# Modulation vectors of a two-block model: from products on TensorE to multiply-adds on VectorE

## The chip, the cores and the metric

The kernel runs on one core of a Trainium2 chip. A core has TensorE (matrix products into PSUM), VectorE, ScalarE, GpSimd, and SyncE, whose queue issues the loads. The metric is device time in microseconds, the median of several runs; lower is better.

## The reference, cut to what matters

The model is a first block (feed-forwards, an mLSTM mixer, dilated attention, all on 512 tokens of width 1024) and a second block of two layers. Each layer of the second block begins with a modulation that depends on two vectors alone, `c` for the latent tokens and `c_ctx` for the 256 context tokens:

```python
shift, scale, gate       = split(silu(c)     @ w_mod + b_mod, 3)   # w_mod: [1024, 3072] per layer
shift_c, scale_c, gate_c = split(silu(c_ctx) @ w_mod + b_mod, 3)
h_lat = x   * (1 + scale[:, None]) + shift[:, None]
h_ctx = ctx * (1 + scale_c) + shift_c
...                                    # projections, recurrence, two attentions: y_l, y_c
x   = layer_norm(alpha * x   + gate[:, None] * y_l)
ctx = layer_norm(alpha * ctx + gate_c * y_c)     # layer 0 only
```

So per layer a 1024 x 3072 matrix is multiplied by two vectors, in float32: 12 MB are loaded for 2 x 3072 numbers.

## The kernel before, in words

**Layout.** Activations lie feature-major, eight tiles of 128 features by 512 tokens (256 for the context). Large projections run on TensorE as three products of 12-bit parts: a weight tile is loaded into a `raw` buffer, ScalarE copies its high part out, VectorE subtracts to get the low part (`loadw`, `split`), and `mm3` issues low x high, high x low, high x high. A feed-forward weight tile of 128x1024 is split in two halves of 512 columns and gives 24 products of 512 columns.

**Order.** The program is recorded first. `par` weaves independent parts: the first feed-forward `ffn(1, 0)` with `ctx_in(0)` (whose first step is `modulation(0)`) and `mem_kv(0)`; the third, `ffn(1, 1)`, with `ctx_in(1)` and `mem_kv(1)`. A list schedule (`schedule`, `simulate`) with an estimated cost per operation then fixes the order of issue on all engines and a numbered buffer per tile, for the whole program at once. Buffers are few: 4 `raw` (4 KB a partition), 70 `t` (2 KB a partition), 8 PSUM banks `ps`. Each engine runs its list in order and waits by semaphores. Every instruction is issued in `emit`, so that the profile shows line 568 for all of them, and they are told apart by tile kind and shape: `raw` <- `in_wmod_dram` is a load of modulation weights, `ps<-raw,const 128*32` a modulation product, `ps<-t,t 128*128 128x512` a feed-forward or projection product.

**The modulation.** `setup2` puts 0.5 (tanh(c/2) + 1) c for both vectors into the first two of 32 columns of `self.sc`, the others being zero. `modulation(l)` takes the 24 tiles of 128x1024 of `w_mod` (three blocks of 1024 columns, eight row tiles each). Blocks 0 and 1 share a PSUM bank, block 2 has its own. Of each row tile the columns are cut into four, and each quarter is a product of its own on one of four column tiles of TensorE:

```python
self.mm(ps[32 * c:32 * c + 32], self.sc[:, k], w[o // 1024][:, o % 1024:o % 1024 + m],
        start=(k == 0), stop=(k == KD - 1))
```

with m = 512 for the first two blocks and 256 for the third. The 32 output rows are c, c_ctx and zeros. ScalarE copies the sums out, TensorE transposes them, VectorE adds `b_mod`.

Of the kernel before, what the change touches and what calls it, by code (L numbers as in the profile page):

```python
# [14 lines left out]
ALU = mybir.AluOpType  # L15
AX = mybir.AxisListType
P = 128
T = 512
KD = 8
# [4 lines left out]
# ------------------------------------------------------------------ host layouts  # L24
# [5 lines left out]
def _wt(w, ksplit=1):  # L30
    """[K, M] -> [M/128, ksplit, 128, K/128/ksplit*128]: one contiguous block per load."""
    k, m = w.shape
    a = w.reshape(ksplit, k // P // ksplit, P, m // P, P).transpose(3, 0, 2, 1, 4)
    return a.reshape(m // P, ksplit, P, -1)


def _wk(w):
    """[K, N] -> [128, K/128*N]: k tiles side by side."""
    k, n = w.shape
    return w.reshape(k // P, P, n).transpose(1, 0, 2).reshape(P, -1)  # L40
# [71 lines left out]
def _rot():  # L112
    """The lhsT of the rope rotation [-x2, x1, -x4, x3] in each half of 64."""
    m = np.zeros((P, P), np.float32)
    for o in (0, 32, 64, 96):
        for j in range(16):
            m[o + 16 + j, o + j] = -1.0
            m[o + j, o + 16 + j] = 1.0
    return m
# [11 lines left out]
def _order(strict):  # L131
    """[128 = (half, beta or eta, i), direction, head parity, chunk of pair, t]: i up to t in the direction's order, in
    the half that holds the chunk; strict: i before t, and eta alone."""
# [28 lines left out]
def _masks():  # L162
    """Selectors of the first block, loaded where they are used."""
# [7 lines left out]
def pack(a):  # L171
    """Lays the inputs out for the chip: permutations, paddings and copies only."""
# [25 lines left out]
    # second block: tiles r3 k3 v3 dd|ad, rg3, aq3, ak, ag3, nq2, nk2, ng2; token-major av|nv  # L198
    q6 = np.arange(384).reshape(6, 64)[[0, 3, 1, 4, 2, 5]].reshape(-1)
    for l in range(2):  # L200
# [9 lines left out]
        # [3 blocks, 8 k tiles, 128, 1024]  # L210
# [22 lines left out]
def _dil_bias(rel):  # L233
    """[4 heads, 128 queries, 512]: previous and own block of group 0, group 1, group 2; entries of rel_bias or NEG."""
# [11 lines left out]
# neighbourhood attention: tokens in the order (column, row); a tile of 128 queries (16 columns) sees 256 keys from here  # L246
# [3 lines left out]
def _na_bias(rpb):  # L250
    """[2 pairs of heads, 4 tiles, 128 queries, 2 x 256 keys]: entries of rpb, or NEG outside the window of columns."""
# [10 lines left out]
# ------------------------------------------------------------------ recording, order and on-chip memory  # L262
# The program is recorded first, as operations on named tiles. A list schedule over estimated times then fixes the
# order in which the operations are issued, and for every tile one of the numbered slots of its kind.
# [27 lines left out]
class Ref:  # L292
    """A recorded tile, or a view of it. v: numbers of the cells it covers, a cell being a column of 32 partitions."""
# [43 lines left out]
class Recorder:  # L337
    """Stands for the NeuronCore: notes (engine, method, arguments) in the current list."""
# [15 lines left out]
class Op:  # L354
# [9 lines left out]
    def _cost(self):  # L364
        """Estimated microseconds on the engine."""
# [25 lines left out]
def weave(parts):  # L391
    """One order for independent lists of operations, each spread evenly by cost."""
# [9 lines left out]
def dependences(ops):  # L402
    """For each operation the earlier ones that it has to follow."""
    writer, readers, last_pe = {}, {}, {}     # per tile: the last writer of each cell; reads since: (operation, cells)
# [36 lines left out]
def simulate(ops, before, after, key, lag, ahead):  # L441
    """A list schedule: of the operations that are ready and whose tiles have slots, each engine takes the one of least
    key. Only the one of least key overall may take the last slots. lag(i, j): time from the end of i to the start of j."""
# [6 lines left out]
    empty = {k: [(0.0, i) for i in range(m)] for k, m in SLOTS.items()}     # (time, slot) of free slots  # L450
    ready, free = [0.0] * n, dict.fromkeys(ENGINES, 0.0)
    wait = {e: [] for e in ENGINES}       # (time, operation): inputs complete at a later time
    can = {e: [] for e in ENGINES}        # (key, operation)
# [6 lines left out]
    def room(i, tight):  # L460
        """When the slots that operation i needs are free; None if there are none."""
# [67 lines left out]
def schedule(ops):  # L529
    """The order of issue, and a slot per tile: a schedule made from the end gives the latest start of each operation;  # L530
    one from the front takes the operations by that. Each further round makes the schedule from the end by the last one
    from the front."""
# [19 lines left out]
def emit(tc, ops):  # L552
    """Issues the recorded operations through Tile."""
# [17 lines left out]
# ------------------------------------------------------------------ the program  # L571
class Prog:
# [13 lines left out]
    # ---- memory  # L586
# [9 lines left out]
    def t2(self, shape=(P, T), dt=F32):  # L596
        """A tile of up to 2 KB a partition; two small ones from the same place in the program share a slot."""
# [28 lines left out]
    # ---- order  # L626
    def par(self, *parts):
        """Independent parts of the program, woven together."""
# [9 lines left out]
    # ---- small helpers  # L638
# [29 lines left out]
    def tr(self, out, a):  # L668
        """PE transpose of 128 partitions, exact."""
        self.nc.tensor.transpose(out, a, self.idn)  # L670

    def split(self, h, l, src, scale=None):
        """src (times a per-partition scale) as the exact sum of two 12-bit parts."""
# [7 lines left out]
    def loadw(self, src, n, w):  # L681
        """n columns of weights as parts, a pair per w columns."""
# [15 lines left out]
    def proj(self, src, xh, xl, n=T, cut=None):  # L698
        """One feature-major tile: out[m, t] = sum_d w[d, m] x[d, t]; cut: ranges of tokens, one after the other."""
# [7 lines left out]
    def proj_tm(self, src, ncol, xh, xl, sels):  # L707
        """Token-major: out[t, n] = sum_d x[d, t] w[d, n]; src [128, 8*ncol], k tiles side by side."""
# [8 lines left out]
    def pow(self, out, a):  # L717
        """out = a ** -0.5."""
# [4 lines left out]
    def rsqrt(self, out, src, n, scale, eps):  # L723
        """out = (src * scale + eps) ** -0.5 for n columns."""
# [4 lines left out]
    def sums(self, tiles, nt):  # L729
        """PSUM [128 = i, t, 2 j + h] = sum over half h of the partitions of tiles[j][:, (t, i)]; the tokens' blocks are  # L730
        summed side by side on the tensor engine."""
# [7 lines left out]
    def turn(self, ps, nt):  # L739
        """PSUM [32 nt, 128] transposed, [128, nt, 32]."""  # L740
# [6 lines left out]
    def parts(self, n=T, cnt=KD):  # L747
        """cnt pairs of [128, n] tiles for the parts of a split."""
# [7 lines left out]
    def norm(self, src, gain, n=T):  # L756
        """The parts of gain*x, and the sum over feature tiles of x**2 / 1024."""
# [13 lines left out]
    def norm_r(self, acc, n=T, bcast=True, step=1):  # L771
        """The rms factors: r (tokens on partitions; every step-th token in a tile), R (on all partitions)."""
# [13 lines left out]
    def bcast(self, R, r, nt):  # L786
        """R[p, (t, i)] = r[i, t]: a column per token tile spread over all partitions."""
# [5 lines left out]
    def heads(self, r, nt):  # L793
        """PSUM [128 = 2 heads x 64, (t, i)] = r[i, t, head]; r: [128, nt, 2]."""
# [7 lines left out]
    # ---- feed-forward  # L802
# [30 lines left out]
    # ---- memory keys and values of one layer (they depend on mem alone)  # L833
# [26 lines left out]
    def knorm(self, kk, nh):  # L860
        """kk [128, nh, 64] *= rsqrt(mean(kk**2) + eps) per head, in place."""
# [8 lines left out]
    def qstat(self, qT, nt):  # L870
        """qT: feature-major tiles [128 = 2 heads x 64, n]. Returns r [128, nt, heads]: rsqrt(mean(q**2) + eps)."""
# [10 lines left out]
    def mem_attn(self, qT, KT, V):  # L882
        """qT: two raw query tiles [128 = 2 heads x 64, 512]. Returns PSUM tiles [128 = 2 heads x 64, 512]."""
# [44 lines left out]
    # ---- layer 0 mixer  # L928
    def mlstm(self, KT, V):
# [3 lines left out]
        # gates first: their chain is the longest  # L933
# [1144 lines left out]
```

## Time and profile before

| | us |
|---|---|
| median of 3 runs | 3384.07 |
| lowest and highest | 3383.62, 3389.64 |
| the profiled execution, span | 3384.7 |
| TensorE busy (matmul) | 3282.6, 97% |
| VectorE busy | 2188.4, 65% |
| ScalarE busy | 1611.1, 48% |
| GpSimd busy | 241.4, 7% |
| mean granted TensorE clock | 0.987 |

The profiled execution is one run with the hardware's records on. Its time is its span; the busy times are shares of that. Busy records of TensorE overlap, since products are pipelined; in the timeline a row gives the start of a series of like instructions, how long it lasts, and its count.

### The profile page before, as it was taken

What the parts mean: (1) busy time and instruction counts of PE and PEld (TensorE: products, weight loads), DVE (VectorE), ACT (ScalarE), POOL (GpSimd) and SP (SyncE); (2) the same over time, 40 slices, a digit from 0 to 9 for tenths busy, and PEclk for the clock granted to TensorE, in tenths of its full rate; (3) what the DMA queues carried; (4) which work ended last, traced back from release to release, by engine and by line L of the source; (5) the groups of instructions that cost most, each with busy time, mean ns of one, the idle gap of its engine ahead of it and who ended that gap; (6) DMA issues with size and microseconds to landing.
All of it is one profiled execution on the core that took longest, in us unless ns stands there. A gap on an engine that the chain in (4) does not pass through costs nothing.

```text
span 3384.7 us, 55344 instructions
## 1 busy us (share of the span) xinstructions
PE 3282.6 (97%) x21302; PEld 2604.3 (77%) x21302; DVE 2188.4 (65%) x4605; ACT 1611.1 (48%) x3577; POOL 241.4 (7%) x233
## 2 busy tenths in 40 slices
PE   8999999999999999999999999999999898999898
PEld 4688878878877788767887788777777677877677
DVE  5455578475578676444567846677575787585876
ACT  3333455363434345322345735343553873654773
POOL 0000000000000101000001000000121011010101
PEclk9999999999999999999999999999999999999999
DMA  6434433123222333444332332223322233322231
GB/s 212 152 122 130 138 102 107 53 81 108 93 68 88 110 127 117 138 137 132 95 105 74 116 95 89 72 89 107 111 72 81 73 113 101 109 85 87 60 119 47
DMA packets 153489, 348.41 MB, mean 103 GB/s; under 512 B 16645, under 2 KB 60421, under 8 KB 153225
## 3 DMA queue, kind: packets, MB, share of 16 engines
q1 hardware_dynamic: 153224, 344.87, 32.0%
q8 instruction: 167, 2.74, 0.3%
q14 instruction: 98, 0.79, 0.1%
HBM read 315.05 MB, written 29.76 MB: 102 GB/s over the span
## 4 chain that ended last, share of the span: by engine, by line
PE 84%; DVE 7%; ACT 5%; issue 1%; DMA 1%; POOL 1%; SPq 0%; ACTq 0%; POOLq 0%; DVEq 0%
PE ps L568 84%; DVE t L568 5%; ACT t L568 4%; ACT big L568 1%; DVE big L568 1%; DVE s L568 1%; DVE tmp L568 1%; POOL s L568 1%; DMA raw<-in_wgu_dram 1%; ACT uv L568 0%; DMA raw<-in_aw_dram 0%; DMA raw<-in_win_dram 0%; DMA raw<-in_wmod_dram 0%; DVE uv L568 0%; SPq L568 0%
## 5 line engine op out<-in xcount | busy, mean ns | idle before, releaser
L568 PE MATMUL ps<-t,t 128*128 128x512 f32 (+6 forms) x15204 | 2880.3, 352 | 48.2 <-ACT t L568 26.3
L568 PEld LDWEIGHTS ps<-t,t 128*128 128x128 f32 (+2 forms) x15204 | 2282.3, 182 | 549.9 <-issue 93.1
L568 ACT ACTIVATE t<-raw 128x512 fp32r<-128x512 f32 (+1 forms) x962 | 565.0, 612 | 777.3 <-PE ps L568 526.1
L568 DVE TENSOR_TENSOR t<-raw,t 128x512 fp32r<-128x512 f32 (+2 forms) x962 | 626.2, 671 | 295.8 <-PE ps L568 197.4
L568 ACT ACTIVATE t<-t 128x512 f32<-128x512 f32 (+8 forms) x739 | 376.8, 525 | 448.1 <-DVE t L568 251.6
L568 DVE TENSOR_TENSOR t<-t,t 128x256 f32<-128x256 f32 (+7 forms) x812 | 417.8, 544 | 110.7 <-ACT t L568 62.5
L568 DVE TENSOR_TENSOR t<-ps,t 128x512 f32<-128x512 f32 (+3 forms) x274 | 178.9, 658 | 236.7 <-PE ps L568 229.3
L568 ACT ACTIVATE t<-ps 128x512 f32<-128x512 f32 (+9 forms) x446 | 215.0, 513 | 233.2 <-PE ps L568 230.6
L568 POOL TENSOR_TENSOR s<-s,const 128x4 f32<-128x4 f32 (+6 forms) x65 | 99.3, 1530 | 1788.9 <-DVE s L568 1780.6
L568 DVE SCALAR_TENSOR_TENSOR t<-ps,t 128x512 f32<-128x512 f32 (+3 forms) x229 | 148.1, 649 | 106.1 <-PE ps L568 105.2
L568 PE MATMUL ps<-const,t 128*128 128x128 f32 (+1 forms) x1116 | 188.0, 289 | 20.3 <-ACT t L568 11.8
L568 PEld LDWEIGHTS ps<-const,t 128*128 128x128 f32 x1116 | 134.7, 147 | 64.8 <-ACT t L568 27.9
L568 PE MATMUL ps<-uv,t 64*64 64x64 f32 (+1 forms) x2208 | 143.9, 229 | 3.4 <-DVE t L568 1.6
L568 PEld LDWEIGHTS ps<-uv,t 64*64 64x64 f32 (+1 forms) x2208 | 103.3, 135 | 53.0 <-issue 14.4
L568 ACT ACTIVATE t<-t,const 128x256 f32<-128x256 f32 (+3 forms) x165 | 102.0, 645 | 68.8 <-DVE t L568 37.2
L568 ACT ACTIVATE uv<-ps 32x128 f32<-32x128 f32 (+1 forms) x288 | 92.2, 321 | 59.4 <-PE ps L568 55.3
L568 DVE SCALAR_TENSOR_TENSOR t<-t,t 128x512 f32<-128x512 f32 (+2 forms) x116 | 76.6, 662 | 57.6 <-ACT t L568 56.3
L568 DVE TENSOR_TENSOR uv<-uv,ps 32x192 f32<-32x192 f32 x192 | 66.6, 347 | 66.3 <-PE ps L568 58.7
L568 POOL TENSOR_TENSOR S<-S,s 128x192 f32<-128x192 f32 x96 | 62.4, 650 | 601.0 <-DVE S L568 451.7
L568 PE MATMUL ps<-S,t 64*32 64x64 f32 x2112 | 104.1, 224 | 1.0 <-DVE S L568 1.0
L568 ACT ACTIVATE t<-ps,s,s 128x256 f32<-128x256 f32 (+1 forms) x140 | 88.2, 652 | 32.8 <-DVE s L568 32.7
L568 ACT ACTIVATE t<-ps,const 128x256 f32<-128x256 f32 (+1 forms) x100 | 57.1, 576 | 75.6 <-PE ps L568 74.9
(81 smaller groups left out, 1390.4 us busy)
## 6 DMA issues: line engine op xcount, KB each, us to landing
raw<-in_wgu_dram SPq DMA_DIRECT2D x176, 512.0 KB, 3.8
raw<-in_win_dram SPq DMA_DIRECT2D x88, 512.0 KB, 3.7
raw<-in_wd_dram SPq DMA_DIRECT2D x128, 256.0 KB, 2.7
raw<-in_wmod_dram SPq DMA_DIRECT2D x48, 512.0 KB, 3.8
t<-dram SPq DMA_DIRECT2D x68, 256.0 KB, 3.0
dram<-t SPq DMA_DIRECT2D x68, 256.0 KB, 2.0
t<-dram SPq DMA_DIRECT2D x97, 128.0 KB, 2.3
raw<-in_wd_dram SPq DMA_DIRECT2D x64, 192.0 KB, 2.4
```

The lines of the kernel that those rows point to most:

```text
L568: getattr(getattr(tc.nc, op.eng), op.method)(*map(real, op.a), **{q: real(v) for q, v in op.k.items()})
```

## The change

The sum over the eight row tiles moves to VectorE. Each 128x1024 tile of `w_mod` is multiplied, partition by partition, by that tile's column of silu(c) and added to a running tile; the same for c_ctx; in two halves of 512 columns, so that four `t` tiles hold the sums of a block. The first row tile is a `tensor_scalar` (a scaling), the other seven are `scalar_tensor_tensor` (a multiply-add). What is left is the sum over the 128 partitions, which TensorE does with a 128x32 matrix `pick[:, v]` that is one in column v and zero elsewhere, so that c comes out in row 0 and c_ctx in row 1 of each column tile. The three blocks are now treated alike, 256 columns on each column tile. Comments and docstrings are also gone from the file, which moves line numbers.

```diff
 def setup2(self):
...
-        self.sc = self.const([P, KD, 32])
-        nc.vector.memset(self.sc, 0.0)
-        self.ts(self.sc[:, :, 0:2], sc.rearrange("p a k -> p k a"), 0.5, ALU.mult)
+        self.sc = self.const([P, KD, 2])
+        self.ts(self.sc, sc.rearrange("p a k -> p k a"), 0.5, ALU.mult)
+        self.pick = self.const([P, 2, 32])
+        nc.vector.memset(self.pick, 0.0)
+        for v in range(2):
+            nc.vector.memset(self.pick[:, v, v:v + 1], 1.0)
...
 def modulation(self, l):
-        for b0, nb in ((0, 2), (2, 1)):
-            m = 256 * nb
+        m, nh = 256, 2
+        for b in range(3):
+            acc = [[self.t2() for _ in range(2)] for _ in range(2)]
+            for k in range(KD):
+                w = self.load(self.new("raw", (P, 1024)), self.I[f"wmod{l}"][b, k])
+                for v in range(2):
+                    for h in range(2):
+                        a, x, c = acc[v][h], w[:, T * h:T * h + T], self.sc[:, k, v:v + 1]
+                        if k == 0:
+                            self.ts(a, x, c, ALU.mult)
+                        else:
+                            self.stt(a, x, c, a, ALU.mult, ALU.add)
             ps = self.ps((P, m))
-            for k in range(KD):
-                w = [self.load(self.new("raw", (P, 1024)), self.I[f"wmod{l}"][b0 + b, k]) for b in range(nb)]
-                for c in range(4):
-                    o = c * m
-                    self.mm(ps[32 * c:32 * c + 32], self.sc[:, k], w[o // 1024][:, o % 1024:o % 1024 + m],
-                            start=(k == 0), stop=(k == KD - 1))
+            for c in range(4):
+                for v in range(2):
+                    self.mm(ps[32 * c:32 * c + 32], self.pick[:, v], acc[v][c // 2][:, m * (c % 2):m * (c % 2) + m],
+                            start=(v == 0), stop=(v == 1))
...
```

The whole program is scheduled anew. Three places show it. The first is TensorE early in the first feed-forward, with the third block of layer 0's modulation in `ps_709`, its weights in `raw_643`, and the feed-forward's sums in `ps_696`; before:

```order
L568 MATMUL ps_709<-raw_643,const_92 32x256
L568 MATMUL ps_696<-t_444,t_646 128x512
L568 MATMUL ps_696<-t_538,t_652 128x512
L568 MATMUL ps_696<-t_543,t_646 128x512
L568 MATMUL ps_709<-raw_643,const_92 32x256
L568 MATMUL ps_696<-t_538,t_646 128x512
L568 MATMUL ps_696<-t_617,t_652 128x512
L568 MATMUL ps_696<-t_623,t_646 128x512
L568 MATMUL ps_709<-raw_643,const_92 32x256
```

After, the first block of layer 0 on TensorE (`ps_643` its bank, `t_178`, `t_180` the sums for c, `t_184`, `t_190` those for c_ctx, `const_94` the pick matrix):

```order
L568 MATMUL ps_592<-t_199,t_564 128x512
L568 MATMUL ps_643<-t_178,const_94 32x256
L568 MATMUL ps_643<-t_184,const_94 32x256
L568 MATMUL ps_643<-t_178,const_94 32x256
L568 MATMUL ps_643<-t_184,const_94 32x256
L568 MATMUL ps_643<-t_180,const_94 32x256
L568 MATMUL ps_643<-t_190,const_94 32x256
L568 MATMUL ps_643<-t_180,const_94 32x256
L568 MATMUL ps_643<-t_190,const_94 32x256
L568 MATMUL ps_658<-t_377,t_638 128x512
```

The products that stood between feed-forward products for each row tile are gone, and eight of a block stand together. All six blocks make 48 such products, in 13 groups.

The second place is VectorE while the feed-forward's second to fourth weight tiles are split (the subtractions that read `raw_245` and `raw_291` are splits; `raw_226`, `raw_259` and `raw_326` hold modulation weights; `const_130` is silu of the two vectors); after:

```order
L568 SCALAR_TENSOR_TENSOR t_190<-raw_226,const_130,t_190 128x512
L568 TENSOR_TENSOR t_299<-raw_245,t_279 128x512
L568 SCALAR_TENSOR_TENSOR t_178<-raw_259,const_130,t_178 128x512
L568 SCALAR_TENSOR_TENSOR t_180<-raw_259,const_130,t_180 128x512
L568 SCALAR_TENSOR_TENSOR t_184<-raw_259,const_130,t_184 128x512
L568 TENSOR_SCALAR s_77_305<-ps_301 128x4
L568 TENSOR_TENSOR t_332<-raw_245,t_284 128x512
L568 SCALAR_TENSOR_TENSOR t_190<-raw_259,const_130,t_190 128x512
L568 TENSOR_TENSOR t_356<-raw_291,t_317 128x512
L568 TENSOR_TENSOR t_367<-raw_291,t_328 128x512
L568 SCALAR_TENSOR_TENSOR t_178<-raw_326,const_130,t_178 128x512
```

Four multiply-adds per modulation tile now stand between the splits; before, the splits of two tiles followed each other with only the feed-forward's own work between them. The 96 scalings and multiply-adds of layer 0 end before the third block's products on TensorE, which stand at its 529th to 542nd row.

The third place is SyncE's queue from its seventh load on, at the start of the program (`in_x_dram` is the input, `in_wgu_dram` the feed-forward's weights; five tiles of x stand ahead in both); of before and after:

```order
L568 DMA raw_137<-in_wgu_dram 128x1024
L568 DMA raw_149<-in_wmod_dram 128x1024
L568 DMA raw_161<-in_wmod_dram 128x1024
L568 DMA t_174<-in_x_dram 128x512
L568 DMA t_180<-in_x_dram 128x512
L568 DMA t_189<-in_x_dram 128x512
```

```order
L568 DMA raw_140<-in_wmod_dram 128x1024
L568 DMA t_152<-in_x_dram 128x512
L568 DMA t_161<-in_x_dram 128x512
L568 DMA t_166<-in_x_dram 128x512
L568 DMA raw_176<-in_wgu_dram 128x1024
L568 DMA raw_188<-in_wmod_dram 128x1024
L568 DMA raw_203<-in_wgu_dram 128x1024
```

The first weights of the feed-forward move from ahead of two modulation tiles to behind one of them and the rest of x.

## Rows read from the trace of the kernel before

**Rows 1.** The page's first part: busy us, share of the span, instructions.

```profile
PE 3282.6 (97%) x21302; PEld 2604.3 (77%) x21302; DVE 2188.4 (65%) x4605; ACT 1611.1 (48%) x3577; POOL 241.4 (7%) x233
```

**Rows 2.** The chain that ended last, by engine.

```profile
PE 84%; DVE 7%; ACT 5%; issue 1%; DMA 1%; POOL 1%; SPq 0%; ACTq 0%; POOLq 0%; DVEq 0%
```

**Rows 3.** Stretches: length, busy us of PE, PEld, DVE, ACT, POOL, clock, DMA.

```profile
11.00:170.00 159.00, 158.98 (x664) 98.52 (x665) 75.91 (x132) 56.84 (x111) 2.03 (x2) 1.00 0.53 177
1366.00:1580.00 214.00, 214.00 (x887) 144.05 (x886) 96.87 (x158) 60.04 (x109) 3.97 (x3) 1.00 0.43 134
...
1800.00:1900.00 100.00, 93.97 (x658) 69.34 (x657) 82.79 (x252) 77.16 (x220) 12.06 (x4) 0.98 0.15 48
```

**Rows 4.** TensorE's groups by form, modulation products: busy us, mean ns, idle before.

```profile
L568 PE MATMUL ps<-raw,const 128*32 128x512 f32 x128 | 48.9, 619 | 11.0 <-DMA raw<-in_wmod_dram 11.0
...
L568 PE MATMUL ps<-raw,const 128*32 128x256 f32 x128 | 25.5, 391 | 0.0
```

**Rows 5.** Timeline of TensorE, layer 0: start us, length us, instruction, count.

```profile
24.40 1.05 PE L568 MATMUL ps<-raw,const 128*32 128x512 f32 x4
...
31.17 1.07 PE L568 MATMUL ps<-raw,const 128*32 128x512 f32 x8
...
84.53 1.04 PE L568 MATMUL ps<-raw,const 128*32 128x512 f32 x2
85.50 0.96 PE L568 MATMUL ps<-t,t 128*128 128x512 f32 x3
86.40 1.04 PE L568 MATMUL ps<-raw,const 128*32 128x512 f32 x2
...
92.84 0.62 PE L568 MATMUL ps<-raw,const 128*32 128x256 f32 x2
...
105.11 0.62 PE L568 MATMUL ps<-raw,const 128*32 128x256 f32 x2
105.66 0.96 PE L568 MATMUL ps<-t,t 128*128 128x512 f32 x3
...
139.84 20.33 PE L568 MATMUL ps<-t,t 128*128 128x512 f32 x95
...
166.78 0.64 PE L568 MATMUL ps<-raw,const 128*32 128x256 f32 x8
```

**Rows 6.** Timeline of TensorE, layer 1: first and last group of each width.

```profile
1366.68 1.05 PE L568 MATMUL ps<-raw,const 128*32 128x512 f32 x4
...
1493.93 1.04 PE L568 MATMUL ps<-raw,const 128*32 128x512 f32 x2
...
1505.40 0.62 PE L568 MATMUL ps<-raw,const 128*32 128x256 f32 x2
...
1578.14 0.64 PE L568 MATMUL ps<-raw,const 128*32 128x256 f32 x8
```

**Rows 7.** Timeline of TensorE at the start of the program.

```profile
11.02 1.89 PE L568 MATMUL ps<-raw,const 128*32 128x512 f32 x2 [11.02 <-DMA raw<-in_wmod_dram]
12.84 0.80 PE L568 MATMUL ps<-t,t 128*128 128x512 f32 x1
...
23.39 0.42 PE L568 MATMUL ps<-t,const 128*32 128x128 f32 x8
```

**Rows 8.** VectorE's groups by form, operations with a column as scalar.

```profile
L568 DVE SCALAR_TENSOR_TENSOR t<-t,const,t 128x512 fp32r<-128x512 f32 x56 | 41.0, 748 | 6.1 <-ACT t L568 4.7 <-PE ps L568 1.2
...
L568 DVE TENSOR_SCALAR t<-t,const 128x512 f32<-128x512 f32 x12 | 5.7, 480 | 0.1
```

**Rows 9.** Timeline of VectorE, a multiply-add and what follows without a wait.

```profile
727.30 0.75 DVE L568 SCALAR_TENSOR_TENSOR t<-t,const,t 128x512 fp32r<-128x512 f32 x1
727.97 1.28 DVE L568 TENSOR_TENSOR t<-raw,t 128x512 fp32r<-128x512 f32 x2
```

**Rows 10.** The page's DMA issues: count, size, median us to landing.

```profile
raw<-in_wmod_dram SPq DMA_DIRECT2D x48, 512.0 KB, 3.8
```

**Rows 11.** Waits: engine, for whom, us in total, times, longest.

```profile
ACT t L568 <- DMA raw<-in_wgu_dram: 75.6, 44, 5.5
```

More of the change, by code (lines that the diff above doesn't have):

```diff
@@ L1360, in modulation @@
         mod = self.const([P, 24, 2])
-        for b0, nb in ((0, 2), (2, 1)):
-            m = 256 * nb
-            ps = self.ps((P, m))
-            for k in range(KD):
-                w = [self.load(self.new("raw", (P, 1024)), self.I[f"wmod{l}"][b0 + b, k]) for b in range(nb)]
-                for c in range(4):
-                    o = c * m
-                    self.mm(ps[32 * c:32 * c + 32], self.sc[:, k], w[o // 1024][:, o % 1024:o % 1024 + m],
-                            start=(k == 0), stop=(k == KD - 1))
+        m, nh = 256, 2
[10 more added lines that the diff above has]
+                            self.stt(a, x, c, a, ALU.mult, ALU.add)
+            ps = self.ps((P, m))
+            for c in range(4):
+                for v in range(2):
+                    self.mm(ps[32 * c:32 * c + 32], self.pick[:, v], acc[v][c // 2][:, m * (c % 2):m * (c % 2) + m],
+                            start=(v == 0), stop=(v == 1))
             row = self.t2((P, m))
             self.act(row, ps)
-            nh = m // P
             pm = self.ps((P, nh, 4, 32))
@@ L1376, in modulation @@
                 self.tr(pm[:, h].rearrange("p c t -> p (c t)"), row[:, P * h:P * h + P])
-            o, n = 8 * b0, 8 * nb
-            self.tt(mod[:, o:o + n].rearrange("p (c h) w -> p c h w", c=4), pm[:, :, :, 0:2].rearrange("p h c w -> p c h w"),
-                    self.c(f"bmod{l}", o, n).rearrange("p (c h) -> p c h", c=4).unsqueeze(3).to_broadcast([P, 4, nh, 2]), ALU.add)
+            o = 8 * b
+            self.tt(mod[:, o:o + 8].rearrange("p (c h) w -> p c h w", c=4), pm[:, :, :, 0:2].rearrange("p h c w -> p c h w"),
+                    self.c(f"bmod{l}", o, 8).rearrange("p (c h) -> p c h", c=4).unsqueeze(3).to_broadcast([P, 4, nh, 2]), ALU.add)
         self.ts(mod[:, 8:16], mod[:, 8:16], 1.0, ALU.add)
```

## Prediction

> **What bounds the kernel now.** I read the busy times of the engines first, then the chain that ended last, then the stretches in which the modulation runs, and inside them the timelines of TensorE and VectorE. TensorE is busy 3282.6 of 3384.7 us, VectorE 2188.4 [rows 1], and the chain runs over TensorE for 84% of the span [rows 2]. The modulation's products lie in two stretches, 11 to 170 us (layer 0, beside the first feed-forward) and 1366 to 1580 us (layer 1, beside the third). There TensorE has no idle time worth a name (158.98 of 159.00 and 214.00 of 214.00 us), its granted clock is 1.00, the 2.4 GHz level, and VectorE is busy 75.91 and 96.87 us [rows 3].
>
> Busy need not mean bound, so I looked at the rate: 95 feed-forward products of 512 columns in a row take 20.33 us [rows 5], 0.214 us each, which is 512 columns at 2.4 GHz with nothing between them. So in these stretches each microsecond that TensorE is relieved of should come off the end.
>
> The Trainium skill speaks against this reading ("Perfetto Trace Analysis", "Identifying the Most-Contended Engine"): a matmul's busy share is a poor measure and the share of weight loads should be used instead. That share is 77% for TensorE here, so by the rule it would have a quarter of its time free and the change would bring nothing; the 0.214 us do not agree with it, and it is kept as rival D.
>
> **What is removed.** 128 float32 products with 32 output rows, 64 of 512 columns and 64 of 256, each with two records [rows 4]. Their records say 48.9 + 25.5 us, but the timeline shows a higher price. A group of them that stands between feed-forward products holds TensorE from its start to the start of the next product: 0.97 us for 512 columns (84.53 to 85.50), 0.55 for 256 (105.11 to 105.66), and it matters little how many of the four column tiles are in a group (1.04 us busy for two records, 1.07 for eight) [rows 5]. Behind it the feed-forward is slow to start: three products take 0.90 us (85.50 to 86.40) where 3 x 0.214 = 0.64 would do. That is 0.26 us a group. So a group costs 1.23 us or 0.81 us.
>
> Groups in the timeline: in layer 0, 17 of 512 columns from 24.40 to 86.40 us and 21 of 256 from 92.84 to 166.78 (of each kind the first and the last stand in [rows 5]); in layer 1, 24 from 1366.68 to 1493.93 and 20 from 1505.40 to 1578.14 [rows 6]. Layer 0: 17 x 1.23 + 21 x 0.81 = 37.9 us. Layer 1: 24 x 1.23 + 20 x 0.81 = 45.7 us. Together 83.6 us. The four groups before 24 us stand in the start and are counted there.
>
> **The start.** Before, TensorE waits 11.02 us for the first modulation weights and its first feed-forward product starts at 12.84; 24 of these are done when 23.39 comes [rows 7]. After, the queue of loads puts one modulation tile and all of x ahead of the first feed-forward weights, 1.25 MB more than before, and VectorE does four scalings before it splits them. Against that, no modulation products stand among the first 24. Before, the 2.4 MB up to the first modulation tile are there at 11.02 us, some 2 us of which pass before the first load lands; so 1.25 MB are 4 to 5 us, the first product starts near 17, and 24 x 0.214 = 5.1 us end near 22. Value -1 us, between -4 and +4.
>
> **What TensorE still does.** Per layer three blocks of eight products of 256 columns, two on each of four column tiles. The two records of such a product stream for 0.97 - 0.55 = 0.42 us (the difference between the two widths is another 256 columns), and a group has 0.13 us of start and 0.26 us of restart. No row shows two products that follow one another on the same column tile with another tile's behind them. If the four tiles run side by side, a block is 2 x 0.42 + 0.39 = 1.23 us; if all eight stand in line, 8 x 0.42 + 0.39 = 3.75. In the order of issue (tile 0 twice, tile 1 twice, ...) only the neighbour can overlap: five steps, 2.49 us. I take that: 6 x 2.49 = 15, and as the order cuts the six blocks into 13 groups, 7 x 0.39 = 3 more: 18 us, between 10 and 25.
>
> The Trainium skill ("TensorEngine Tiling (Array Packing)", "Key Properties") says that tiles work independently of each other. By that the blocks would take the lower end and the sum would be 8 us better; the eight records in 1.07 us agree for one product per tile, and nothing here shows it for two.
>
> **What VectorE gets.** Per block 4 scalings and 28 multiply-adds on 128x512. A scaling by a column is 0.480 us; a multiply-add with a column as scalar has 0.748 us in its records [rows 8], but back to back the next one starts 0.67 us later (727.30 to 727.97) [rows 9]. A block is 4 x 0.48 + 28 x 0.67 = 20.7 us, a layer 62.0 us, the program 124 us.
>
> Layer 1: 96.87 + 62 = 159 us of VectorE work in 214 - 45.7 + 9 = 177 us of TensorE work, 90%. Layer 0: 75.91 + 62 = 138 us in 159 - 37.9 + 9 = 130 us. So in layer 0 VectorE does not cover: it also splits each weight tile for the feed-forward, and TensorE cannot start a tile before its split. The order agrees: all 96 operations of layer 0 lie between the splits of the feed-forward's first tiles, up to the row of TensorE that the old products also reached. The excess is 8 us; what slides out of the stretch lowers it, waits inside VectorE's queue raise it. I take 10 us for layer 0 and 2 for layer 1, between 4 and 26.
>
> Three copies out of PSUM per layer in place of two, and one more addition, are far from the path. The rest of the program is planned anew as well, since one list schedule covers it; TensorE's idle time in all is 102 us [rows 1], and if a tenth of that comes or goes it is 10 us either way, value 0.
>
> **Sum.** -83.6 - 1 + 18 + 12 = -54.6 us, from the profiled execution's 3384.7 us: 3330 us. Its span is 0.6 us above the median of the runs (3384.07), so nothing lies around it that would have to be added. All ends together: 3301 to 3366.
>
> **Rivals.**
> A, the forecast: TensorE's time counts, VectorE takes back a part. 3330.
> B, VectorE becomes the bound. For it: the 138 us in 130, and that VectorE's fullest stretch that I found has 82.79% busy, with TensorE at 94% in it [rows 3]. If it gets no further, layer 0 needs 138 / 0.83 = 166 us, 36 us too many, and layer 1 191, 14 too many: 50 us in place of 12, 3368 us. Against it: that stretch has 252 small instructions, 0.33 us each, whereas the multiply-adds are twice as long and ready as soon as their tile is there, so that they can fill gaps.
> C, slower: the buffers for raw weights. There are four; a modulation tile now holds one until its fourth multiply-add is through VectorE's queue, in which splits stand, and before only until four products were done. Each such load lands 3.8 us after issue [rows 10]. If each of the 48 tiles delays the feed-forward's next weights by 1.1 us, (83.6 - 1 - 18 - 12) / 48, the gain is gone; at half a landing, 1.9 us, the kernel takes 3330 + 91 = 3421 us. For it: ScalarE already waited 75.6 us for these weights, up to 5.5 us at once [rows 11]. Against it: that wait was hidden in a TensorE without gaps, and loads of the two kinds alternate in the queue.
> D, TensorE's busy time is no bound, and its relief is lost in other waits: 3385 us. The rate in [rows 5] speaks against it.
> E, the picks overlap fully and VectorE's gaps take the additions: -83.6 - 3 + 10 + 4 = -73, and less by the new plan: about 3305 us.
>
> **How the numbers follow.** A 0.60, B 0.17, C 0.08, D 0.05, E 0.10. The time is A's, 3330. The range is 3302 to 3366: it holds A, most of E and two thirds of B. About 0.2% (7 us) is what a measurement can tell from no change. Faster: A, E and nearly all of B, 0.86; the same: D and a little of B, 0.06; slower: C, 0.08.
>
> **What would show it.** The stretch of layer 0: VectorE above 95% busy there and TensorE with gaps that end on VectorE's splits, about 10 us in sum; if there are none, the 12 us were too many, if over 35, B. The picks: eight-product blocks of some 2.5 us; 1.2 shows E, 3.7 the serial case. The first feed-forward product: near 17 us. Up to the end of the first feed-forward about 20 us should be gained (37.9 + 1 - 9 - 10), in the third about 35 (45.7 - 9 - 2). ScalarE's waits for weights grow only in C, with TensorE waiting behind it. The prediction is wrong if the stretches are shorter and the end is not.

## The result and the profile after

The changed kernel takes 3325.97 us (median of four runs, 3325.18 to 3327.22), the kernel before beside it 3385.33: a ratio of 0.982, 95% interval 0.981 to 0.984, or 59.4 us less. The forecast was 3330, 54.6 less. The profiled execution spans 3325.4 us at a mean granted clock of 0.987, as before, so the difference is not one of the clock.

The first part of the page after the change, to be read against [rows 1]:

```profile
PE 3217.1 (97%) x21142; PEld 2604.3 (78%) x21142; DVE 2299.8 (69%) x4801; ACT 1613.3 (49%) x3579; POOL 252.0 (8%) x233
```

TensorE's busy time falls by 65.5 us, nearly what the span loses, and VectorE's grows by 111.4. TensorE is still the busiest at 97%. By the rule weighed in the prediction (the Trainium skill, "Perfetto Trace Analysis", "Identifying the Most-Contended Engine"), the 77% share of weight loads would have left TensorE slack; the measurement differs, since relief of TensorE came off the end.

Where in the program did the time go? No product tells it, because all are planned anew. The loads of two weight tensors make good markers: the mixer output weights of layer 0 and of layer 1 are fetched after the stretches with the modulation, at the same point of the work in every kernel. The DMA issues of these two, before (count, ns of one issue, first to last start in us):

```profile
L568 SPq DMA_DIRECT2D raw<-in_awo_dram x8: 327/328/382, 627.3 to 718.2; - x8
...
L568 SPq DMA_DIRECT2D raw<-in_bwo_dram x8: 327/328/333, 1809.7 to 1898.2; - x8
```

and after:

```profile
L568 SPq DMA_DIRECT2D raw<-in_awo_dram x8: 328/328/382, 600.3 to 689.7; - x8
...
L568 SPq DMA_DIRECT2D raw<-in_bwo_dram x8: 327/328/333, 1752.6 to 1841.9; - x8
```

Read at the last load: 718.2 to 689.7 is 28.5 us gained in layer 0. From there to 1898.2 is 1180.0 us before and 1152.2 after: 27.8 us gained in layer 1. What is behind is 3.0 us shorter by the spans. So 56.3 of the 59.3 us lie up to the two markers, half in each layer.

The stretches themselves, which answer to [rows 3] (length, busy us of PE, PEld, DVE, ACT, POOL, clock, DMA share, GB/s):

```profile
11.00:130.00 119.00, 114.42 (x524) 92.59 (x524) 116.94 (x197) 44.31 (x83) 1.40 (x1) 1.00 0.63 214
...
1340.00:1520.00 180.00, 180.00 (x809) 144.36 (x808) 125.89 (x208) 59.87 (x108) 3.14 (x2) 1.00 0.42 135
```

In layer 0 VectorE is 98% busy (116.94 of 119 us), and yet TensorE lacks only 4.58 us, all of it at the front, up to its first product. In layer 1 TensorE has no gap at all, with VectorE 70% busy.

TensorE's timeline after, which answers to [rows 5] and [rows 7]: the start, then a whole block of eight picks, and one that the plan cut in two:

```profile
15.58 10.83 PE L568 MATMUL ps<-t,t 128*128 128x512 f32 x36 [15.58 <-DVE t L568]
26.33 0.42 PE L568 MATMUL ps<-t,const 128*32 128x128 f32 x8
...
128.87 1.09 PE L568 MATMUL ps<-t,const 128*32 128x256 f32 x16
129.89 0.50 PE L568 MATMUL ps<-t,t 128*128 128x512 f32 x1
137.90 0.62 PE L568 MATMUL ps<-t,const 128*32 128x256 f32 x2
138.45 1.42 PE L568 MATMUL ps<-t,t 128*128 128x512 f32 x5
```

The eight picks, as the products with the pick matrix are called (16 records), hold TensorE from 128.87 to 129.89, 1.02 us; with the prediction's 0.26 us of restart that is 1.28, not 2.49. A single pick (2 records) holds it 0.55 us, the price of an old group of that width. The rule on independent tiles ("Key Properties", in the Trainium skill's "TensorEngine Tiling (Array Packing)") was right here: the trace now shows it for two products per tile.

VectorE's multiply-adds as a group, to be read against [rows 8] (busy us, mean ns, idle before):

```profile
L568 DVE SCALAR_TENSOR_TENSOR t<-raw,const,t 128x512 f32<-128x512 f32 x168 | 117.9, 744 | 1.4 <-DMA raw<-in_wmod_dram 1.4
```

and in its timeline:

```profile
10.06 1.67 DVE L568 TENSOR_SCALAR t<-raw,const 128x512 f32<-128x512 f32 x4
...
14.84 1.28 DVE L568 TENSOR_TENSOR t<-raw,t 128x512 fp32r<-128x512 f32 x2
...
21.71 2.72 DVE L568 SCALAR_TENSOR_TENSOR t<-raw,const,t 128x512 f32<-128x512 f32 x4
24.36 0.68 DVE L568 TENSOR_TENSOR t<-raw,t 128x512 fp32r<-128x512 f32 x1
```

Four multiply-adds take 2.65 us (21.71 to 24.36), 0.66 each, as estimated from [rows 9]. They waited 1.4 us for data in the whole program. Ahead of the first split, at 14.84, VectorE has four scalings of modulation work. TensorE's waits for VectorE up to 130 us (total, times, longest) are the one before its first product:

```profile
PE ps L568 <- DVE t L568: 15.6, 1, 15.6
```

ScalarE's wait for feed-forward weights in the whole program, of [rows 11], is in sum no longer than it was:

```profile
ACT t L568 <- DMA raw<-in_wgu_dram: 74.2, 40, 6.9
```

### The profile page after: what moved, and what is told of

The parts are those of the page before. It is cut to its first block, busy times and chain, and to the rows that moved or that the text cites. A ratio compares the mean times of both kernels' runs of the same rounds, so it can differ in the third digit from the quotient of the medians.

```text
span 3325.4 us, 55255 instructions
## 1 busy us (share of the span) xinstructions
PE 3217.1 (97%) x21142; PEld 2604.3 (78%) x21142; DVE 2299.8 (69%) x4801; ACT 1613.3 (49%) x3579; POOL 252.0 (8%) x233
## 5 line engine op out<-in xcount | busy, mean ns | idle before, releaser
L568 ACT ACTIVATE t<-ps 128x512 f32<-128x512 f32 (+8 forms) x448 | 216.0, 511 | 219.5 <-PE ps L568 214.6
L568 POOL TENSOR_TENSOR s<-s,const 128x4 f32<-128x4 f32 (+6 forms) x65 | 110.2, 1698 | 1722.4 <-DVE s L568 1714.0
L568 PEld LDWEIGHTS ps<-const,t 128*128 128x128 f32 x1116 | 137.4, 149 | 66.1 <-ACT t L568 27.8
L568 ACT ACTIVATE uv<-ps 32x128 f32<-32x128 f32 (+1 forms) x288 | 92.5, 322 | 59.4 <-PE ps L568 55.4
L568 DVE SCALAR_TENSOR_TENSOR t<-raw,const,t 128x512 f32<-128x512 f32 x168 | 117.9, 744 | 1.4 <-DMA raw<-in_wmod_dram 1.4
L568 ACT ACTIVATE t<-ps,s,s 128x256 f32<-128x256 f32 (+1 forms) x140 | 88.1, 650 | 26.4 <-DVE s L568 26.3
```

Of the source, the lines that this page charges most:

```text
L568: getattr(getattr(tc.nc, op.eng), op.method)(*map(real, op.a), **{q: real(v) for q, v in op.k.items()})
```

## The experiments

The theory: the gain is what TensorE no longer issues, counted in groups (1.23 and 0.81 us each), less the groups of picks, less what VectorE cannot hide. The main rival: the groups cost little or nothing, and the gain is that of another plan. A second question was how much VectorE's 112 us of multiply-adds (168 x 0.67) cost. Each kernel ran five rounds beside the kernel before (medians 3385.5, 3389.6, 3388.7 and 3386.7 in the four sets); ratios are to that.

**Fewer groups, same work (e1_unit).** The kernel before, in which the four products of a row tile enter the plan as one unit, so that nothing can stand between them. VectorE gets nothing.

```
-                for c in range(4):
-                    o = c * m
-                    self.mm(ps[32 * c:32 * c + 32], self.sc[:, k], w[...], start=(k == 0), stop=(k == KD - 1))
+                self.nc.tensor.many(*[(ps[32 * c:32 * c + 32], dict(lhsT=self.sc[:, k], rhs=w[...],
+                                       start=(k == 0), stop=(k == KD - 1))) for c in range(4)])
```

> The kernel before, with the four products of a row tile issued as one unit on TensorE (8 groups of 512 columns and 8 of 256 per layer in place of 21 and 21, or 24 and 20); VectorE gets nothing. Theory (TensorE pays per group, 1.23 us for 512 columns and 0.81 for 256): the modulation costs 16 x 1.23 + 16 x 0.81 = 33 us in place of 84, so 3385 - 51 = 3334 us, within 12. Rival (TensorE pays for the columns that it streams, so only taking products away helps): no change, 3385 us.

Measured: 3337.26 us, 0.9858 (0.9844 to 0.9871), 48 us less. Its timeline on TensorE:

```profile
32.92 1.06 PE L575 MATMUL ps<-raw,const 128*32 128x512 f32 x8
33.92 6.42 PE L575 MATMUL ps<-t,t 128*128 128x512 f32 x27
...
76.93 0.64 PE L575 MATMUL ps<-raw,const 128*32 128x256 f32 x8
77.50 2.79 PE L575 MATMUL ps<-t,t 128*128 128x512 f32 x11
```

All four tiles together take 1.00 and 0.57 us, what one product took in [rows 5]. Thus the group is the unit of price, and the same 128 products cost 48 us less when they stand together. Four fifths of the gain are to be had with no work moved to VectorE.

**Only the last row tile (e11_last).** As above, but the products of the other seven row tiles are left out (their weights are loaded and not used); four groups remain. This is the change without picks and without VectorE's part.

```
-                for c in range(4):
...
+                if k == KD - 1:
+                    self.nc.tensor.many(... start=True, stop=True) ...
```

> The kernel before with only the products of the last of the eight row tiles, as one unit per bank (4 groups in all); the other row tiles are loaded and not used, so the modulation is not the whole sum. It prices the products taken away, with nothing on VectorE. Theory (84 us for all groups, 4 left at 1.23 or 0.81): 3386 - 84 + 4 = 3306 us, within 12. Rival (the groups cost only what their records say, 74 us less what lies in waits, say 50): 3336.

Measured: 3302.40 us, 0.9749 (0.9736 to 0.9763), 86 us less. Its markers and the start of its TensorE:

```profile
L575 SPq DMA_DIRECT2D raw<-in_awo_dram x8: 327/328/382, 587.4 to 677.9; - x8
...
L575 SPq DMA_DIRECT2D raw<-in_bwo_dram x8: 327/328/333, 1716.0 to 1820.1; - x8
```

```profile
9.72 10.56 PE L575 MATMUL ps<-t,t 128*128 128x512 f32 x37 [9.72 <-DVE t L575]
20.21 0.43 PE L575 MATMUL ps<-t,const 128*32 128x128 f32 x8
```

Layer 0 is 40.3 us shorter than before, layer 1 37.8. With the two units that each layer keeps (1.23 + 0.81 = 2.04), the removal is worth 42.3 and 39.8 us, 82.1 together. In layer 0 this holds the four groups that stood in the start. The other 8.7 us by which the span is shorter lie behind layer 1's marker and are no price of groups. e1_unit says nearly the same by another way: its markers give 24.5 and 26.3 us, and its 16 units a layer cost 8 x 2.04 = 16.3, so 40.8 and 42.6, 83.4 together.

**One layer at a time (e2_layer0, e3_layer1).** The new modulation in one layer, the old one in the other.

```
+        if l != 0:      # e3_layer1: if l != 1
+            return self.modulation_old(l)
```

> The changed modulation in layer 0, the old one in layer 1. By the prediction's sum layer 0 brings 37.9 + 1 - 9 - 10 = 20 us: 3365. If VectorE takes back next to nothing there, 30 us: 3355. Rival (the gain is luck of the new plan and does not belong to the layers): a gain outside 10 to 40 us, and together with the run for layer 1 not 59 us.

> The changed modulation in layer 1, the old one in layer 0. By the prediction's sum layer 1 brings 45.7 - 9 - 2 = 35 us: 3350. If VectorE takes back as much here as in layer 0 (10 us or more), 27 us: 3358. Rival (luck of the plan): outside 20 to 45 us.

Measured: layer 0 alone 3358.13, 0.9917 (0.9903 to 0.9931), 27.4 less; layer 1 alone 3352.60, 0.9899 (0.9885 to 0.9912), 32.9 less. The sum, 60.3, is the whole change's 59.4: the two add up, and neither lives from the other.

**Multiply-adds cut to one column (e4_noadd).** The 168 instructions stay, but work on one column of 512.

```
-                            self.stt(a, x, c, a, ALU.mult, ALU.add)
+                            self.stt(a[:, :n], x[:, :n], c, a[:, :n], ALU.mult, ALU.add)   # n = 1
```

> The changed kernel, with seven of eight multiply-adds of each sum cut to one column of 512, so that the sums hold only the first row tile elsewhere; loads and TensorE's products stay. Theory (VectorE's additions take back 12 us of what TensorE gains): 3326 - 12 = 3314 us, within 8. Rival 1 (they are hidden): 3326. Rival 2 (VectorE is the bound in both stretches, 30 us or more): 3296 or below.

Measured: 3327.86, 0.9824 (0.981 to 0.9837), no gain on the change at all. This one misled. Freed of VectorE, the plan scattered the picks over about 25 groups where the change has 13, and a dozen more groups at 0.8 us are about the 10 us that VectorE could have given back. Two costs had moved at once, so it settles nothing; the next two have six groups each.

**Picks as a unit (e6_pickunit), and the same with the multiply-adds cut (e7_noadd_unit).** The eight picks of a block enter the plan as one unit: six groups in place of 13.

```
-            for c in range(4):
-                for v in range(2):
-                    self.mm(ps[32 * c:32 * c + 32], self.pick[:, v], ..., start=(v == 0), stop=(v == 1))
+            self.nc.tensor.many(*[(ps[32 * c:32 * c + 32], dict(lhsT=self.pick[:, v], rhs=...,
+                                   start=(v == 0), stop=(v == 1))) for c in range(4) for v in range(2)])
```

> The changed kernel with the eight last products of a block issued as one unit: 6 groups on TensorE in place of 13. In the changed kernel's timeline 13 groups stand, ten of 1.23 us and three of 0.81: 14.7 us; six make 7.4. Theory (TensorE pays per group): 3326 - 7 = 3319 us, within 6. Rival (these few products lie in gaps that TensorE has anyway while it waits for VectorE): 3326.

> As the run before, and the multiply-adds after the first row tile cut to one column of 512 in both layers, so that the sums are not the whole sums. The run without the additions alone had its last products scattered over some 25 groups, so that it did not isolate VectorE; here they are six in both. Theory (VectorE's additions take back 12 us): 3319 - 12 = 3307, within 6. Rival (the additions are hidden): 3319 as the run before.

Measured: the unit 3319.86, 0.9799 (0.9786 to 0.9813), 6 us below the change by medians and 7.9 by spans; 14.7 - 7.7 = 7.0 was to be had by the prices above. (With another plan the same step brought less, see the last experiment.) With the multiply-adds cut 3316.14, 0.9789 (0.9774 to 0.9805): 3.7 us less again by medians, 7.1 by spans. The intervals overlap, so what 112 us of multiply-adds cost is small: 4 and 7 us by these two readings, and by medians not told from nothing. In the trace it looks like this. TensorE in the unit kernel:

```profile
16.79 8.96 PE L575 MATMUL ps<-t,t 128*128 128x512 f32 x32 [16.79 <-DVE t L575]
25.68 0.43 PE L575 MATMUL ps<-t,const 128*32 128x128 f32 x8
...
63.51 1.09 PE L575 MATMUL ps<-t,const 128*32 128x256 f32 x16
64.53 0.97 PE L575 MATMUL ps<-t,t 128*128 128x512 f32 x3
```

and with the multiply-adds cut:

```profile
10.45 11.29 PE L575 MATMUL ps<-t,t 128*128 128x512 f32 x37 [10.45 <-DVE t L575]
21.66 0.43 PE L575 MATMUL ps<-t,const 128*32 128x128 f32 x8
...
62.83 0.44 PE L575 MATMUL ps<-const,t 128*128 128x128 f32 x2 [2.39 <-ACT t L575]
```

At the start the multiply-adds cost some 4 us (25.68 against 21.66, and five fewer products done); after that the cut kernel loses 2.39 us to a wait of its own, for ScalarE. Not all of the 4 us is VectorE's time, since the order of the loads differs too. The first feed-forward weights are issued at 6.20 us in the unit kernel and at 2.59 in the cut one:

```profile
6.20 0.61 SPq L575 DMA_DIRECT2D raw<-in_wgu_dram  x1
```

```profile
2.59 0.43 SPq L575 DMA_DIRECT2D raw<-in_wgu_dram  x1
```

At the marker of layer 0 only 1.6 us are left of it (688.3 and 686.7), in layer 1 4.6 (1146.0 and 1141.4).

**Each multiply-add twice (e10_double).** The unit kernel with a second multiply-add into a spare tile behind each: 112 us more on VectorE.

```
                             self.stt(a, x, c, a, ALU.mult, ALU.add)
+                            self.stt(spare, x, c, a, ALU.mult, ALU.add)
```

> As the unit run, with each multiply-add done twice, the second into a tile that nobody reads: 56 us more on VectorE per layer. Theory (VectorE is full in layer 0's stretch and has 10% left in layer 1's): layer 0 pays most of the 56 us unless its additions slide out of the stretch, layer 1 some 37: 3319 + 60 = 3380 us, within 30. Rival (the schedule slides the additions into the later, emptier part of the feed-forward, which has 45% of VectorE free): 3319 to 3330.

Measured: 3345.83, 0.9873 (0.986 to 0.9887): 26 us above the unit kernel, 23% of the added work. That is less than the theory's lower end and more than nothing, so neither expectation held. The stretches of the unit kernel:

```profile
11.00:130.00 119.00, 113.10 (x519) 91.91 (x523) 117.48 (x197) 45.58 (x86) 1.40 (x1) 1.00 0.66 212
130.00:400.00 270.00, 269.91 (x1380) 223.78 (x1371) 154.16 (x282) 109.43 (x216) 6.52 (x6) 1.00 0.43 134
```

and of the doubled one:

```profile
11.00:130.00 119.00, 98.40 (x417) 76.79 (x418) 117.17 (x193) 38.85 (x74) 1.46 (x1) 0.96 0.48 156
130.00:400.00 270.00, 269.83 (x1368) 225.61 (x1367) 192.76 (x337) 102.88 (x195) 6.17 (x5) 1.00 0.46 144
```

VectorE is as full in the first stretch as it was (117.17 against 117.48), and 38.6 us more of its work lie between 130 and 400 us, where TensorE has no gap (269.83 of 270). In the first stretch TensorE loses 14.7 us. TensorE's waits for VectorE up to 130 us (total, times, longest) in the doubled kernel say where:

```profile
PE ps L575 <- DVE t L575: 31.6, 5, 21.2
```

The first product waits 21.2 us, where the unit kernel's waits 16.79, and four more waits make 10.4 us. The granted clock of that stretch is 0.96 and not 1.00. So an excess of VectorE is paid in part in the stretch, and the rest slides into a later one that has room. By the markers the doubled kernel loses 17.3 us in layer 0 (705.6 against 688.3) and 9.0 in layer 1 (1155.0 against 1146.0).

**The load ahead of the modulation (e12_late).** The unit kernel; silu(c) is made to wait for the split of the first feed-forward weight tile, so that this tile is first in the queue of loads and the modulation starts behind it.

```
+        self.first = self.loadw(I["wgu10"][0, 0], 1024, P)
...
+        self.ts(half, self.first[0][1].bitcast(F32)[:, 0:1], 0.0, ALU.mult, 0.5, ALU.add)
...
+        self.ts(self.sc, sc.rearrange("p a k -> p k a"), half, ALU.mult)
```

> The changed kernel with the last products as units (3320 us), and silu(c) made to wait for the split of the feed-forward's first weight tile, whose load so comes ahead of x and of all modulation tiles. In the unit run the first 36 feed-forward products are done at 25.7 us, with the additions cut at 21.7, and with nearly no modulation at 20.2. Theory (what VectorE takes back in layer 0 is mostly the start, where the first split stands behind modulation work): 36 products done at 21 to 23 us, the kernel at 3316, within 4. Rival (the full stretch behind the start decides, so time won at the start is lost again by 130 us): 3320, and the last mixer weights of the first block issued at 688 us as before.

Measured: 3312.50 (3311.09 to 3318.63), 0.9785 (0.9772 to 0.9799). The start:

```profile
7.16 7.07 PE L575 MATMUL ps<-t,t 128*128 128x512 f32 x16 [7.16 <-ACT t L575]
...
20.24 4.44 PE L575 MATMUL ps<-t,t 128*128 128x512 f32 x12 [3.05 <-DVE t L575]
24.62 0.43 PE L575 MATMUL ps<-t,const 128*32 128x128 f32 x8
```

and a stretch of it, in the columns of [rows 3]:

```profile
20.00:22.00 2.00, 1.76 (x4) 1.47 (x5) 2.00 (x5) 0.96 (x3) 0.00 (x0) 0.50 0.09 23
```

The first product starts at 7.16 us and not at 16.79, but TensorE then waits for splits, 3.05 us before 20.24, and the row that ends the start comes at 24.62, 1.1 us sooner than in the unit kernel: the time at the front is not set by the first load alone. The wait has a second price: behind it the granted clock is 0.50, the 1.2 GHz level, and twelve products take 4.38 us, 0.36 each. The total falls into the theory's band, but the 36 products are done at 24.62 us and not at 21 to 23, so the theory of the start is not borne out. Layer 0's marker is 3.5 us sooner (684.8). It is the fastest kernel here with the whole computation, 13 us below the change by medians, but its interval and the unit kernel's overlap.

**A new plan alone (c1_plan, c2_plan, c3_planunit).** One constant of the planner is changed, in the kernel before, in the changed one and in the unit kernel. This moves work everywhere and nothing else.

```
-STAY = 2.0
+STAY = 1.9
```

> The kernel before, with one constant of the planner (the 2.0 us for which an engine stays with what it can do at once) set to 1.9: same operations, another order. It tells what a new plan alone does. Theory (a new plan moves the time by up to 10 us): 3375 to 3395. Rival (a new plan alone can bring tens of us, so the gains of the other runs may be luck): outside these.

> The changed kernel with the planner's constant 1.9 in place of 2.0: same operations, another order. The same edit to the kernel before cost it 12 us. Theory (a new plan moves the time by about that): 3314 to 3340. Rival (the gain of the change is the luck of one plan): above 3350.

> The changed kernel with the last products as units (3320 us) and the planner's constant 1.9: whether the 6 us between unit and no unit hold in another plan. Theory (fewer groups): 4 to 10 us below the run beside it with the same constant. Rival (plan luck): not below it.

Measured: before 3401.52, 1.0037 (1.0024 to 1.0049); changed 3343.07, 0.9871 (0.9857 to 0.9884); unit 3333.61, 0.9841 (0.9828 to 0.9855). All three are 12 to 17 us slower than with the old constant, more than I had expected for the first two. Yet the gain of the change hardly depends on it: 3401.5 to 3343.1 are 58.4 us, with the old constant 59.4. What the picks as a unit bring is less firm. By medians it is 9.5 us under the new constant (6.1 under the old), but by the markers only 1.2 us of it lie up to layer 1's marker (7.6 under the old), though the groups are again six in place of 13. Layer 1's marker in the unit kernel under the old constant and under the new one, to be read against 1841.9 and 1843.1:

```profile
L575 SPq DMA_DIRECT2D raw<-in_bwo_dram x8: 328/328/333, 1745.0 to 1834.3; - x8
```

```profile
L575 SPq DMA_DIRECT2D raw<-in_bwo_dram x8: 327/328/333, 1752.1 to 1841.9; - x8
```

The markers of the changed kernel under the new constant:

```profile
L568 SPq DMA_DIRECT2D raw<-in_awo_dram x8: 327/328/371, 600.8 to 690.2; - x8
...
L568 SPq DMA_DIRECT2D raw<-in_bwo_dram x8: 327/328/333, 1753.2 to 1843.1; - x8
```

Up to 1843.1 us it is 1.2 us behind; the other 13 us by spans (3339.7 against 3325.4) come after it. Two stretches there, in the changed kernel:

```profile
2400.00:2500.00 100.00, 94.79 (x723) 76.90 (x722) 74.37 (x160) 58.05 (x123) 22.69 (x14) 0.97 0.24 82
...
2600.00:2700.00 100.00, 88.60 (x928) 71.25 (x928) 86.96 (x222) 85.11 (x215) 6.97 (x8) 0.95 0.28 83
```

and under the new constant:

```profile
2400.00:2500.00 100.00, 90.67 (x644) 72.46 (x643) 71.92 (x152) 52.25 (x110) 17.55 (x14) 0.93 0.21 68
...
2600.00:2700.00 100.00, 90.17 (x902) 69.24 (x900) 84.02 (x212) 81.90 (x207) 6.71 (x8) 0.91 0.25 76
```

Both show a lower granted clock and fewer products in the same 100 us. Whether the wait comes first and the clock follows, or the other way, was not separated.

## Why the prediction was right, point by point

**The bound.** Right, with one row misread. TensorE's relief came off the end, 56.3 of 59.3 us of it up to the two markers, and the group as the unit of price held: e1_unit took 48 us off with the same products, e11_last 78 up to its markers with four groups left. Rival D is out. The misread row is the run of 95 products. A timeline row names the shape of its first product, and by shape the run, here its records between 140 and 160 us, holds both widths:

```profile
L568 PE MATMUL ps<-t,t 128*128 128x512 f32 x82 | 19.2, 389 | 0.0
L568 PE MATMUL ps<-t,t 128*128 128x256 f32 x13 | 2.0, 282 | 0.0
```

A run of 512 columns alone goes slower; in the changed kernel 281 take 63.92 us, 0.227 each and not 0.214:

```profile
64.95 63.99 PE L568 MATMUL ps<-t,t 128*128 128x512 f32 x281
```

So the 0.214 us that seemed to match 2.4 GHz exactly were a chance of the mixture, and a restart is 0.90 - 3 x 0.227 = 0.22 us, not 0.26. e1_unit and e11_last carry the bound without it.

**The removal, 83.6 us.** Too large by about 8, the first term that was mis-sized. The 82 to 83 us measured by two kernels seem to confirm it, but they hold the four groups of the start, which the 83.6 leave out. In e11_last 37 products are done at 20.21 us, so 24 of them near 17.2, against 23.39 before: 6.2 us of layer 0's 42.3 are the start. What is left is 36.1 us in layer 0, where I had 37.9, and 39.8 in layer 1, where I had 45.7 (e1_unit gives 42.6 there): 75.9 in all. With the restart at 0.22 us the 38 and 44 groups come to 36.4 and 44.0, so layer 0 is explained; why layer 1's cost less still, I did not find out.

**The start, -1 us.** Near, by one offset. The first product comes at 15.58 us, not 17, but the first 36 then take 10.75 us, 0.30 each; 24 of them are done near 26.33 - 12 x 0.227 = 23.6, against 23.39 before [rows 7], 0.2 us later. The step that failed is "24 x 0.214": in the trace the first products, which end TensorE's 15.58 us of idleness, start 0.43 us apart up to 20.44 us, and only then 0.23. VectorE's multiply-adds do not make this, since in e11_last, which has none, the first 37 take 10.49 us. Before, too, the first group held TensorE 1.82 us (11.02 to 12.84 [rows 7]) where later ones took 0.97. The spacing of 0.43 us is 512 columns at 1.2 GHz, and the profile's record of the granted clock begins, at 1.00, at 20.6 us (13.3 in e11_last), just where the spacing changes; the clock before that is not recorded, so that it is the cause is likely and not shown.

**The picks, 18 us.** Too many by 3. The step that failed is "only the neighbour can overlap: five steps, 2.49 us": a block takes 1.28. The count of 13 groups was right, and it, not the streaming, makes the price: 10 groups at about 1.23 us and 3 at 0.81 are 14.7 us, 5.7 in layer 0 and 9.0 in layer 1. Six units cost 7.7. These are prices times counts; e6_pickunit's 7.6 us by the markers agree with them, the 1.2 us under the other plan do not.

**VectorE, 12 us.** Too many by about 7, and wrong in kind. What the other terms leave over is 36.1 - 0.2 - 5.7 - 28.5 = 1.7 us in layer 0 and 39.8 - 9.0 - 27.8 = 3.0 in layer 1; e7_noadd_unit puts both together at 4 to 7, with another order of loads in its start, so the two do not check each other closely. What I wrote of the place, gaps of TensorE in layer 0 that end on VectorE's splits, "about 10 us in sum", is not there, and by the prediction's own sign the 12 us were then too many. VectorE is above 95% busy as foretold, but behind the first product TensorE waits for nothing up to 130 us, and its products follow one another at 0.227 us. The plan lets the splits go ahead and the multiply-adds slide; e10_double shows it, and shows that the sum "excess over the stretch" was the wrong model, since the stretch has no hard end for VectorE. The changed kernel's front is 6 us behind that of e11_last (26.33 against 20.21). Only 1.67 us of that are modulation work of VectorE ahead of the first split (the scalings at 10.06). The loads are in another order too, the first feed-forward weights issued at 5.83 us and at 2.59; how the rest divides is not shown.

**By layer, 20 and 35 us.** Wrong: 28.5 and 27.8 by the markers, 27.4 and 32.9 by the two half changes. Layer 0 was set too low by VectorE's 10 us (measured 1.7) and the picks' 9 (5.7), layer 1 too high by the removal, 45.7 against 39.8.

**The new plan, 0 plus or minus 10.** The stretches behind gave 3.0 us. As a bound it was too narrow: c1_plan and c2_plan cost 12 and 17 us.

**The other rivals.** B is out: VectorE could take 98% of the stretch, not 83%, and cutting its work gave 4 to 7 us. C is out: ScalarE's wait is 74.2 us, 75.6 before [rows 11]. E was right on the picks' overlap and on how little VectorE takes back, but not close: with six groups the time is 3320 (e6_pickunit), 15 us above E's 3305, whose removal is the same. The delay at which C would cancel the gain is 54.6 / 48 = 1.14 us, since the start's 1 us belongs to the gain; nothing hangs on it.

**The sum in the sizes measured:** -75.9 (removal) + 0.2 (start) + 14.7 (picks) + 4.7 (VectorE) - 3.0 (behind) = -59.3. The 4.7 are what is left over, so the sum closes by itself. The forecast came within 5 us in part by luck: a removal that was 8 us too large was covered by picks and VectorE that were 11 too costly.

## What to carry to other kernels

Where narrow products stand among a stream of wide ones, count the places where the stream is broken, not the products: put what shares such a break into one unit of the plan before moving work to another engine (48 of the 59 us here; for the picks some 6 more, of which another plan kept little up to the markers). Before calling a second engine the next bound from its share of a stretch, ask whether its work has to end in that stretch. Before taking a rate from a timeline row, ask by shape what the row holds. And when a list schedule covers the program, measure what another plan alone is worth, and read the gain at markers in the stretch that was changed.

## What I had not expected of the hardware

Eight float32 products of 256 columns, two on each of four column tiles and issued tile by tile, hold TensorE 1.02 us, hardly longer than one or four products of 512 columns in a group (0.97 and 1.00 us). The mean granted clock, 0.987 in all four runs of the changed kernel, was 0.980 to 0.982 in the four of c2_plan, with nothing changed but the plan.
